# A hybrid attention and RWKV layer on one core: score pairs as 128-row matmuls with doubled keys, and a top-k search without 16-bit halves, three tiles of it counted on ScalarE

## The chip, the cores and the metric

The kernel runs on one core of one Trainium2 chip. A core has five engines with a queue each: TensorE (PE; PEld is its weight load), VectorE (DVE), ScalarE (ACT), GpSimd (POOL) and SyncE (SP), which issues most DMAs. The metric is device time in microseconds for one execution.

## The reference, cut to what matters

One layer over 1024 prompt frames and 32 sample frames, width 1024. Half of the heads do sparse attention, half RWKV-7; then an output projection and an MLP with 4096 hidden units. What the change touches is the sparse half: an indexer scores each query against the admissible keys, the best 256 keys are kept, and softmax attention runs over these.

```python
dots  = einsum('bthd,bsd->bths', qi, ki_all) * 64 ** -0.5        # 8 indexer heads, 64 wide
score = einsum('bths,bth->bts', relu(dots), wi)
score = where(admissible, score, -inf)                           # chunk-causal
_, idx = top_k(score, 256)
s = einsum('btkgd,btskd->btkgs', q, gathered_keys) * 64 ** -0.5  # 8 heads, 4 key heads
o = einsum('btkgs,btskd->btkgd', softmax(s), gathered_values)
```

## The kernel before

**Precision.** A float32 operand x is split into a high part `hi` (rounded to float32r, the matmul's input type) and a rest `lo = x - hi`; a product needs hi*hi + hi*lo + lo*hi. Head vectors are 64 long, so two of these fit on the 128 rows of the array.

**Tiles.** Tokens are in nine tiles: 0 to 7 are 128 prompt rows each, tile 8 is the 32 sample rows. Tile t has 128(t+1) keys, tile 8 has 544. Tiles 0 and 1 need no search, since all their keys are kept.

**Indexer** (`key_tile`, `key_T`, `cache_keys`, `idx_tile`). `key_T` transposes 64-wide keys and writes the high part to rows 0 to 63 and again to rows 64 to 127 of `kiA`/`ksA`, and the rest to the 64 rows of `kiB`/`ksB`. Queries `qs` hold the high part above the rest. For each of 8 heads and each 512 keys, L324 multiplies 128 rows (`qs` by `kiA`), L325 adds a 64-row matmul (high query by `kiB`); ScalarE applies relu (L326), VectorE weighs and sums over heads into `sc` (L330).

**Top-k search** (`topk`, `count`, `step`). The 256th largest score is found bit by bit: 31 steps, i = 30 to 0. A step counts for each tile how many scores lie below a candidate, then three small VectorE operations (L365, L366, L368) set or clear the bit. The tiles are in two sets, `SLS = ((2,3,4,5,8),(6,7))`, whose steps alternate. The first set is counted on VectorE (L341). The second is counted on VectorE in the 15 upper steps (i >= 16) and by Sign passes with a running sum on ScalarE (L363) in the 16 lower ones; it closes with one more count and two passes that settle the last unit. In the upper steps both sets read `S.upper`, bfloat16 copies of the scores' upper 16 bits (seven copies in `main2`, L519; their space lies in a pool that opens when the indexer's pools have closed).

**Projections beside the search.** `step(1)` advances both sets after each of 18 token tiles (`norm_tile`) and 14 channel blocks (`zs_block`). A channel block is 3 x 24 matmuls of 352 columns (L441) into two accumulators `acc`; ScalarE evacuates each twice (L450, L451); of the third one VectorE first takes two columns into `shl` (L446).

**Attention and RWKV** (`attn_all`, `rwkv_all`, generators that are advanced in turns). For each of 4 key heads and each tile: `prep` (when a new key set begins) transposes keys into `Ks`/`Kp` (high part above the rest), `query` makes `Q` (high part twice) and `Ql` (rest, 64 rows), `scores` does L1107 (128 rows) and L1108 (64 rows), mask and exponent, `turn` transposes the weights, `product` multiplies by values. RWKV's `lane_inverse` is a serial chain of small GpSimd operations (L837, L839).

**Order.** The program order is written by hand through these generators with priorities; a scheduler with a simulated timeline places the instructions in each engine's queue, and an engine takes its queue in order.

Of the kernel before, what the change touches and what calls it, by code (L numbers as in the profile page):

```python
# [74 lines left out]
def rows_of(t):  # L75
    return 128 if t < 8 else 32
# [21 lines left out]
def flat(a):  # L98
    return a.rearrange("p a b -> p (a b)")
# [51 lines left out]
def phase_a(S, pwx, pwy, pa, pi, px, xp, ps, late):  # L151
    nc, I, O = S.nc, S.I, S.O
# [83 lines left out]
    TK = []  # L236
    for SL in SLS:
# [5 lines left out]
        X.off = S.tk.tile([128, 2, len(SL)], F32, name="off" + str(len(SL)))  # L243
    S.upper = None
    ones = S.tk.tile([128, 1], F32, name="ones")
# [3 lines left out]
    kiA = pi.tile([128, 1024], F32R, name="kiA")  # L249
    kiB = pi.tile([64, 1024], F32R, name="kiB")  # L250
    ksA = pi.tile([128, 544], F32R, name="ksA")
    ksB = pi.tile([64, 544], F32R, name="ksB")

    KN = {}

    def key_T(A, B, col, src, r):
        pt = ps.tile([128, 512], F32, name="pt", bufs=2)
        nc.tensor.transpose(pt[:64, :r], src, S.ident[:r, :r])
        nc.scalar.copy(A[0:64, col:col + r], pt[:64, :r])
        nc.scalar.copy(A[64:128, col:col + r], pt[:64, :r])  # L260
        nc.vector.tensor_tensor(B[:, col:col + r], pt[:64, :r], A[0:64, col:col + r].bitcast(F32), op=ALU.subtract)

# [24 lines left out]
    def key_turn(t):  # L287
        r = rows_of(t)
        if t < 8:
            key_T(kiA, kiB, t * 128, KN.pop(t), r)  # L290
        else:
            key_T(ksA, ksB, 512, KN.pop(t), r)

    def cache_keys():
        for c in range(4):
            ck = pa.tile([128, 64], F32, name="ck", bufs=2)
            nc.sync.dma_start(ck, I["cache_kidx"][0, 0, c * 128:(c + 1) * 128])
            key_T(ksA, ksB, c * 128, ck, 128)

    def idx_tile(t, W):  # L300
# [16 lines left out]
        for h in range(8):  # L317
            w = iw[:r, t, h:h + 1]
            rl = late["pj"].tile([128, 1024], F32, name="rl", bufs=2)
            for c0 in range(0, n, 512):  # L320
                c1 = min(n, c0 + 512)
                pd = ps.tile([128, 512], F32, name="pd", bufs=6 - ACB)
                o = pd[:r, :c1 - c0]
                nc.tensor.matmul(o, qs[:, h // 2, h % 2, :r], A[:, c0:c1], start=True, stop=False)  # L324
                nc.tensor.matmul(o, qs[0:64, h // 2, h % 2, :r], B[:, c0:c1], start=False, stop=True)  # L325
                nc.scalar.activation(rl[:r, c0:c1], o, AF.Relu)  # L326
            if h == 0:
                nc.vector.tensor_scalar(sc[:r, :n], rl[:r, :n], w, None, op0=ALU.mult)
            else:
                nc.vector.scalar_tensor_tensor(sc[:r, :n], rl[:r, :n], w, sc[:r, :n], op0=ALU.mult, op1=ALU.add)  # L330
# [13 lines left out]
    def topk(X):  # L344
# [9 lines left out]
        for i in range(30, -1, -1):  # L354

            upper = i >= 16 and S.upper
            if X.exact or upper:
                count(X, ALU.is_lt, c_of, S.upper if upper else S.sc)
            else:
                for j, t in enumerate(X.SL):  # L360
                    r = rows_of(t)
                    n = S.sc[t].shape[1]
                    nc.scalar.activation(junk2[:r, :n], S.sc[t][:r, :n], AF.Sign, bias=c_of(j, r), scale=-1.0,  # L363
                                         accum_out=cnt[:r, j:j + 1])
            nc.vector.tensor_tensor(nac, cnt, X.off[:, 0] if X.exact or upper else X.off[:, 1], op=ALU.is_gt)  # L365
# [61 lines left out]
    def zs_block(i, W, o_, pool, mu1):  # L427
# [5 lines left out]
        for b, (o, n) in enumerate(TB):  # L433
# [10 lines left out]
            with S.tc.high_priority(EVP) if i in EVI else nullcontext():  # L444
                if b == 2:
                    nc.vector.tensor_copy(S.shl[:m, :, zc // 128 + (zc == 1600)], acc[:m, 319:352:32])  # L446
                if b in ZMD:
# [64 lines left out]
    def main2():  # L512
        S.upper, c = {}, 0
        for X in TK:
            for t in X.SL:
                n = S.sc[t].shape[1]
                S.upper[t] = junk2 if t == 7 else S.eqb[:, c:c + n]
                c += n * (t != 7)
                (nc.gpsimd.tensor_copy if t in UPP else nc.scalar.copy)(S.upper[t][:rows_of(t), :n], S.sc[t][:rows_of(t)].bitcast(BF16)[:, 1:2 * n:2])  # L519
        nc.gpsimd.memset(S.shl, 0.0)  # L520
# [531 lines left out]
def attn_all(S, ap, ps):  # L1052
# [6 lines left out]
    def prep(j, samp):  # L1059

        nt, n, sx = (5, 544, "s") if samp else (8, 1024, "p")

        kt, vt = S.kv.pop((j, samp), None) or attn_load(S, j, samp)
        A = ap.tile([128, n], F32R, name="K" + sx, bufs=1)
        for t0 in range(0, nt, 4):
            t1 = min(nt, t0 + 4)
            p = ps.tile([128, 512], F32, name="ptr", bufs=PTB)
            for t in range(t0, t1):
                r = 32 if t == 4 and samp else 128
                nc.tensor.transpose(p[0:64, (t - t0) * 128:(t - t0) * 128 + r], kt[:r, t], S.ident[:r, :r])  # L1070
            m = 32 if t1 == 5 else 512
            c = slice(t0 * 128, t0 * 128 + m)
            nc.scalar.copy(A[0:64, c], p[0:64, :m])
            nc.vector.tensor_tensor(A[64:128, c], p[0:64, :m], A[0:64, c].bitcast(F32), op=ALU.subtract)
        J[j, samp] = A, vt

    def query(k):
# [12 lines left out]
        w.Q = X = ap.tile([128, 2, 128], F32R, name="Q", bufs=2)  # L1090
        w.Ql = Y = ap.tile([64, 2, 128], F32R, name="Ql", bufs=2)
        src = p.rearrange("p (h q) -> p h q", h=2)[:, :, :r]
        nc.scalar.activation(X[0:64, :, :r], src, AF.Copy, scale=0.125)
        nc.scalar.activation(X[64:128, :, :r], src, AF.Copy, scale=0.125)
        nc.vector.scalar_tensor_tensor(Y[:, :, :r], src, 0.125, X[0:64, :, :r].bitcast(F32), op0=ALU.mult, op1=ALU.subtract)

    def scores(k, h):
        j, t = items[k]
        w = W[k]
        r, n, X = w.r, w.n, w.Q  # L1100
        A = J[j, t == 8][0]
        w.s[h] = s = ap.tile([128, 1024], F32, name="s", bufs=XPB)[:r, :n]
        m = w.m[:, h * 3:h * 3 + 2]
        for i, c0 in enumerate(range(0, n, 512)):
            c1 = min(n, c0 + 512)
            pd = ps.tile([128, 512], F32, name="pd", bufs=PDB)[:r, :c1 - c0]
            nc.tensor.matmul(pd, X[:, h, :r], A[:, c0:c1], start=True, stop=False)  # L1107
            nc.tensor.matmul(pd, w.Ql[:, h, :r], A[0:64, c0:c1], start=False, stop=True)  # L1108

# [310 lines left out]
def body(tc, I, O, dbg=None):  # L1420
# [4 lines left out]
    with pool(name="const") as cp, pool(name="dram", space=DRAM) as dp:  # L1425
# [18 lines left out]
        with pool(name="xnt") as xp, pool(name="psA", space=PSUM) as ps:  # L1444
# [103 lines left out]
```

## Time and profile before

| | |
|---|---|
| median of 3 runs | 1850.66 us (1846.62 to 1853.6) |
| profiled execution | 1847.36 us, span 1845.6 us |
| TensorE busy, share of the span | 1716.0 us, 93% |
| VectorE | 986.4 us, 53% |
| ScalarE | 674.8 us, 37% |
| GpSimd | 587.0 us, 32% |
| mean granted TensorE clock | 0.945 of full speed |

The span is from the first to the last instruction of the profiled execution. Busy shares are means over stages with different limits, so each stage is read by itself. "Idle before, releaser" in a group of instructions says what ended the waits of the engine just before them.

### The profile page before, as it was taken

How to read it: one execution, taken by the hardware profiler on the slowest of the kernel's cores; microseconds unless marked ns; L12 is line 12 of the kernel's file. 1: busy time of each engine (PE TensorE's matmuls, PEld its weight loads, DVE VectorE, ACT ScalarE, POOL GpSimd, SP SyncE). 2: the span in 40 equal slices, each digit the busy share in tenths (PEclk: the TensorE clock that was granted, in tenths of full speed). 3: DMA queues.
4: the chain of work that ended last, by engine and by line, in shares of the span. 5: the costliest groups of instructions: out<-in, count | busy, mean ns of one | idle time of the engine just before them, and what ended most of it. 6: DMA issues, size and time to landing. Idle time of an engine off the chain costs nothing.

```text
span 1845.6 us, 29489 instructions
## 1 busy us (share of the span) xinstructions
PE 1716.0 (93%) x11394; PEld 1489.6 (81%) x11394; DVE 986.4 (53%) x2127; ACT 674.8 (37%) x1469; POOL 587.0 (32%) x894
## 2 busy tenths in 40 slices
PE   7999978798669988999899999999999999999999
PEld 6666667797546666666657779999999999999998
DVE  6456599999988777686552543222222222222224
ACT  6455432367635453454641332121212121212120
POOL 7446463244345434055210113121212131313120
PEclk9999988899658897999989999999999999999999
DMA  7111011132311112041212532111111111111105
GB/s 215 47 35 33 33 58 57 54 109 60 89 38 19 27 38 53 14 115 47 60 46 85 155 108 80 40 52 41 52 40 52 41 52 40 52 41 52 41 17 165
DMA packets 180196, 113.08 MB, mean 61 GB/s; under 512 B 51392, under 2 KB 169240, under 8 KB 180056
## 3 DMA queue, kind: packets, MB, share of 16 engines
q1 hardware_dynamic: 171224, 106.87, 20.6%
q10 hardware_dynamic: 8832, 4.33, 0.8%
q8 instruction: 89, 1.46, 0.3%
q14 instruction: 51, 0.42, 0.1%
HBM read 86.16 MB, written 25.01 MB: 60 GB/s over the span
## 4 chain that ended last, share of the span: by engine, by line
PE 66%; DVE 17%; POOL 6%; issue 3%; DMA 3%; ACT 3%; SPq 1%; DVEq 0%; POOLq 0%; ACTq 0%
PE pd L1328 20%; PE pr L1348 10%; DVE AR L341 7%; PE acc L209 5%; PE pc L1348 5%; PE po L1348 5%; PE po L1146 3%; POOL Yl L839 2%; POOL tl L837 2%; PE pd L325 2%; PE pd L1264 2%; PE ptr L1131 2%; DVE L L832 2%; PE pd L1108 1%; PE pd L324 1%
## 5 line engine op out<-in xcount | busy, mean ns | idle before, releaser
L1328 PE MATMUL pd<-hh,w1h 128*128 128x352 f32 x768 | 248.1, 323 | 2.4 <-issue 1.6
L1328 PE MATMUL pd<-hh,w1l 128*128 128x352 f32 x768 | 247.7, 323 | 0.7 <-DVE w1l L1195 0.7
L1328 PE MATMUL pd<-hl,w1h 128*128 128x352 f32 x768 | 247.0, 322 | 0.0
L1334 DVE TENSOR_TENSOR h2l<-rl,h2h 128x352 fp32r<-128x352 f32 x96 | 56.9, 593 | 275.7 <-ACT h2h L1333 275.7
L1332 POOL TENSOR_TENSOR rl<-rl 128x352 f32<-128x352 f32 x96 | 85.2, 888 | 214.0 <-ACT rl L1331 214.0
L1194 ACT CAST w2h<-w2r 128x512 fp32r<-128x512 f32 x64 | 39.7, 621 | 293.6 <-PE po L1348 144.7
L1328 PEld LDWEIGHTS pd<-hh,w1h 128*128 128x128 f32 x768 | 144.3, 188 | 3.0 <-issue 1.9
L1328 PEld LDWEIGHTS pd<-hh,w1l 128*128 128x128 f32 x768 | 144.3, 188 | 0.9 <-DVE w1l L1195 0.9
L1328 PEld LDWEIGHTS pd<-hl,w1h 128*128 128x128 f32 x768 | 144.9, 189 | 0.0
L1195 POOL TENSOR_TENSOR w2l<-w2r,w2h 128x512 fp32r<-128x512 f32 x32 | 41.6, 1299 | 299.8 <-ACT w2h L1194 289.3
L1348 PE MATMUL pr<-h2h,w2l 128*128 128x352 f32 x384 | 124.5, 324 | 0.0
L1348 PE MATMUL pr<-h2h,w2h 128*128 128x352 f32 x384 | 124.4, 324 | 0.0
L1348 PE MATMUL pr<-h2l,w2h 128*128 128x352 f32 x384 | 124.3, 324 | 0.0
L1354 DVE TENSOR_TENSOR ya<-ya,pr 128x352 f32<-128x352 f32 x84 | 43.8, 521 | 100.6 <-PE pr L1348 100.6
L1331 ACT ACTIVATE rl<-pd 128x352 f32<-128x352 f32 x96 | 44.3, 463 | 141.4 <-PE pd L1328 136.1
L1146 PE MATMUL po<-ph,vp 128*64 128x256 f32 x288 | 85.1, 418 | 2.1 <-DVE t L1154 1.6
L1131 PE MATMUL ptr<-ident,s 128*128 128x128 f32 (+2 forms) x328 | 66.6, 308 | 19.0 <-ACT s L1113 17.3
L837 POOL TENSOR_TENSOR tl<-L,Yl 128x56 f32<-128x56 f32 (+22 forms) x155 | 64.4, 416 | 61.6 <-DVE L L832 50.6
L341 DVE TENSOR_SCALAR_CACHE_REDUCE AR<-KB,cnd 128x384 bf16<-128x384 bf16 (+2 forms) x90 | 78.9, 877 | 1.2
L441 PE MATMUL acc<-xh,whx 128*128 128x352 f32 (+2 forms) x168 | 58.4, 348 | 19.3 <-ACT tm L451 12.0
L1333 ACT CAST h2h<-rl 128x352 fp32r<-128x352 f32 x96 | 46.6, 485 | 75.3 <-POOL rl L1332 75.3
L1131 PEld LDWEIGHTS ptr<-ident,s 128*128 128x128 f32 (+2 forms) x328 | 40.5, 155 | 39.9 <-ACT s L1113 18.8
(458 smaller groups left out, 4677.8 us busy)
## 6 DMA issues: line engine op xcount, KB each, us to landing
w1r<-in_w_ff_dram SPq DMA_DIRECT2D x32, 512.0 KB, 4.2
w2r<-in_w_ff_dram SPq DMA_DIRECT2D x64, 256.0 KB, 2.9
zsd<-zm SPq DMA_DIRECT2D x12, 528.0 KB, 3.0
wraw<-in_w_in_dram SPq DMA_DIRECT2D x24, 256.0 KB, 2.7
wraw<-in_w_in_dram SPq DMA_DIRECT2D x40, 128.0 KB, 2.5
x<-in_x_prompt_dram SPq DMA_DIRECT2D x8, 512.0 KB, 5.3
hres<-hd ACTq DMA_DIRECT2D x16, 256.0 KB, 3.0
out_dram<-hres SPq DMA_DIRECT2D x16, 256.0 KB, 2.4
```

What stands on the lines that cost most here:

```text
L209: nc.tensor.matmul(acc[:r, :n], l, w[:, :n], start=(i == 0), stop=(i == 23))
L341: nc.vector.tensor_scalar(junk[:r, :n], sc[t][:r, :n], get(j, r), None, op0=op, op1=ALU.add, accum_out=X.cnt[:r, j:j + 1])
L441: nc.tensor.matmul(acc[:m, :n], l, x, start=(j == 0), stop=(j == 23))
L837: eng.tensor_tensor(t_, L[:, 0:j, j:j + 1].to_broadcast([128, j, w]), Y[:, j:j + 1, m:16].to_broadcast([128, j, w]), op=ALU.mult)
L1131: nc.tensor.transpose(p[:x, i, h, :r], w.s[h][:, c0 + i * 128:c0 + i * 128 + x], S.ident[:r, :r])
L1146: nc.tensor.matmul(po, V[:x, kt], hi[:x, i, :, :r], start=(kt == 0), stop=(kt == w.nk - 1))
L1328: nc.tensor.matmul(acc, a[:, k], m[:, k, o:o + n], start=(i == 0), stop=(i == 23))
L1331: nc.scalar.activation(rl, acc, AF.Relu)
L1332: nc.gpsimd.tensor_tensor(rl, rl, rl, op=ALU.mult)
L1333: nc.scalar.copy(h2h[:, o:o + n], rl)
L1334: nc.vector.tensor_tensor(h2l[:, o:o + n], rl, h2h[:, o:o + n].bitcast(F32), op=ALU.subtract)
L1348: nc.tensor.matmul(acc, a[:, k], m[:, o:o + n], start=(i == 0), stop=(i == 11))
```

## The change

It has five parts. (1) Keys are doubled along the row axis before the transpose (for a computed tile by a GpSimd copy `k2`, for cached indexer keys by a second DMA), so that `kiA`/`ksA` and `K` hold the high part in both halves and `kiB`/`ksB` and `Kl` hold the rest in both halves; the second matmul of a score pair then has 128 rows, with the same stationary operand as the first, and adds rest by rest too. (2) Attention's `Q` holds the high part above the rest, `Ql` and one ScalarE copy go; `K` and `Kl` are one buffer each for sample and prompt. (3) The search reads float32 scores in all steps; `S.upper` and its copies go. (4) Tile 5 moves to the second set, which is counted on ScalarE in all 31 steps. (5) The `shl` copy moves from VectorE to ScalarE.

```diff
     def key_T(A, B, col, src, r):
         pt = ps.tile([128, 512], F32, name="pt", bufs=2)
-        nc.tensor.transpose(pt[:64, :r], src, S.ident[:r, :r])
-        nc.scalar.copy(A[0:64, col:col + r], pt[:64, :r])
-        nc.scalar.copy(A[64:128, col:col + r], pt[:64, :r])
-        nc.vector.tensor_tensor(B[:, col:col + r], pt[:64, :r], A[0:64, col:col + r].bitcast(F32), op=ALU.subtract)
+        nc.tensor.transpose(pt[:, :r], flat(src), S.ident[:r, :r])
+        nc.scalar.copy(A[:, col:col + r], pt[:, :r])
+        nc.vector.tensor_tensor(B[:, col:col + r], pt[:, :r], A[:, col:col + r].bitcast(F32), op=ALU.subtract)
...
     def key_turn(t):
         r = rows_of(t)
+        k2 = pa.tile([128, 2, 64], F32, name="ck", bufs=2)[:r]
+        nc.gpsimd.tensor_copy(k2, KN.pop(t)[:, None, :].to_broadcast([r, 2, 64]))
...
-                nc.tensor.matmul(o, qs[0:64, h // 2, h % 2, :r], B[:, c0:c1], start=False, stop=True)
+                nc.tensor.matmul(o, qs[:, h // 2, h % 2, :r], B[:, c0:c1], start=False, stop=True)
...
         for i in range(30, -1, -1):
-
-            upper = i >= 16 and S.upper
-            if X.exact or upper:
-                count(X, ALU.is_lt, c_of, S.upper if upper else S.sc)
+            if X.exact:
+                count(X, ALU.is_lt, c_of, S.sc)
             else:
...
-                    nc.vector.tensor_copy(S.shl[:m, :, zc // 128 + (zc == 1600)], acc[:m, 319:352:32])
+                    nc.scalar.copy(S.shl[:m, :, zc // 128 + (zc == 1600)], acc[:m, 319:352:32])
...
     def main2():
-        S.upper, c = {}, 0
-        for X in TK:
-            for t in X.SL:
-                n = S.sc[t].shape[1]
-                S.upper[t] = junk2 if t == 7 else S.eqb[:, c:c + n]
-                c += n * (t != 7)
-                (nc.gpsimd.tensor_copy if t in UPP else nc.scalar.copy)(S.upper[t][:rows_of(t), :n], S.sc[t][:rows_of(t)].bitcast(BF16)[:, 1:2 * n:2])
...
-        A = ap.tile([128, n], F32R, name="K" + sx, bufs=1)
+        A, B = [ap.tile([128, 1024], F32R, name=x, bufs=1)[:, :n] for x in ("K", "Kl")]
         for t0 in range(0, nt, 4):
...
+            r = 32 if t0 == 4 and samp else 128
+            k2 = ap.tile([128, 4, 2, 64], F32, name="k2", bufs=1)
+            nc.gpsimd.tensor_copy(k2[:r, :t1 - t0], kt[:r, t0:t1, None, :].to_broadcast([r, t1 - t0, 2, 64]))
             for t in range(t0, t1):
-                r = 32 if t == 4 and samp else 128
-                nc.tensor.transpose(p[0:64, (t - t0) * 128:(t - t0) * 128 + r], kt[:r, t], S.ident[:r, :r])
+                nc.tensor.transpose(p[:, (t - t0) * 128:(t - t0) * 128 + r], flat(k2[:r, t - t0]), S.ident[:r, :r])
...
         nc.scalar.activation(X[0:64, :, :r], src, AF.Copy, scale=0.125)
-        nc.scalar.activation(X[64:128, :, :r], src, AF.Copy, scale=0.125)
-        nc.vector.scalar_tensor_tensor(Y[:, :, :r], src, 0.125, X[0:64, :, :r].bitcast(F32), op0=ALU.mult, op1=ALU.subtract)
+        nc.vector.scalar_tensor_tensor(X[64:128, :, :r], src, 0.125, X[0:64, :, :r].bitcast(F32), op0=ALU.mult, op1=ALU.subtract)
...
-            nc.tensor.matmul(pd, w.Ql[:, h, :r], A[0:64, c0:c1], start=False, stop=True)
+            nc.tensor.matmul(pd, X[:, h, :r], B[:, c0:c1], start=False, stop=True)
...
-SLS = ((2,3,4,5,8),(6,7))
+SLS = ((2,3,4,8),(5,6,7))
```

## Rows read from the trace of the kernel before

**Rows 1.** Six stretches: length, busy time (instructions) per engine, granted clock, DMA share, GB/s.

```profile
84.00:232.00 148.00, 148.00 (x645) 97.67 (x644) 84.29 (x136) 75.02 (x161) 72.49 (x116) 1.00 0.11 31
232.00:358.00 126.00, 98.67 (x494) 89.34 (x493) 124.36 (x324) 30.90 (x66) 55.33 (x68) 0.86 0.19 58
358.00:475.00 117.00, 102.31 (x620) 98.67 (x619) 112.01 (x310) 87.22 (x183) 45.74 (x57) 0.98 0.26 76
475.00:568.00 93.00, 62.69 (x296) 49.51 (x296) 80.83 (x164) 45.48 (x106) 46.72 (x77) 0.56 0.23 59
568.00:1000.00 432.00, 400.29 (x3879) 279.67 (x3879) 285.52 (x657) 206.44 (x502) 146.89 (x305) 0.91 0.19 47
1000.00:1846.00 846.00, 835.99 (x5093) 816.00 (x5091) 253.83 (x426) 184.50 (x337) 169.25 (x153) 1.00 0.22 64
```

Busy times stand in the order PE, PEld, DVE, ACT, POOL.

**Rows 2.** Groups by line and shape, 232 to 475 us: ScalarE's first evacuation.

```profile
L450 ACT ACTIVATE zm<-acc,mu 128x352 f32<-128x352 f32 x36 | 19.7, 548 | 56.5 <-DVE shl L446 35.8 <-PE acc L441 20.7
```

**Rows 3.** Timeline of TensorE's matmuls in the indexer: start, duration, form.

```profile
187.24 0.39 PE L209 MATMUL acc<-wly,xh 128*128 128x512 f32 x1
187.47 0.40 PE L324 MATMUL pd<-kiA,qs 128*128 128x512 f32 x1
187.80 0.49 PE L325 MATMUL pd<-kiB,qs 64*128 64x512 f32 x1
188.22 0.51 PE L209 MATMUL acc<-why,xl 128*128 128x512 f32 x1
188.56 0.40 PE L209 MATMUL acc<-why,xh 128*128 128x512 f32 x1
```

**Rows 4.** Line L325, prompt tiles: durations, first and last start, forms.

```profile
L325 PE MATMUL pd<-kiB,qs x80: 322/492/502, 84.2 to 227.0; 64*128 64x512 f32 x48, 64*128 64x384 f32 x16, 64*128 64x128 f32 x8, 64*128 64x256 f32 x8
```

**Rows 5.** Groups by line and shape, 84 to 232 us: VectorE's widest head sum.

```profile
L330 DVE SCALAR_TENSOR_TENSOR G<-rl,iw,G 128x1024 f32<-128x1024 f32 x7 | 9.9, 1419 | 10.1 <-ACT rl L326 10.1
```

**Rows 6.** VectorE's busy time in counts (L341), sum over 84 to 568 us.

```profile
sum 484.00, DVE 174.36; mean DVE 43.59
```

**Rows 7.** Groups by line and shape, 232 to 475 us: counts, Sign passes, small operations.

```profile
L341 DVE TENSOR_SCALAR_CACHE_REDUCE AR<-AR,cnd 128x1024 bf16<-128x1024 bf16 x15 | 19.1, 1273 | 0.0
L363 ACT ACTIVATE AR<-G,cnd 128x1024 bf16<-128x1024 f32 x16 | 18.4, 1150 | 0.3
L341 DVE TENSOR_SCALAR_CACHE_REDUCE AR<-KB,cnd 128x896 bf16<-128x896 bf16 x15 | 17.0, 1136 | 0.0
L363 ACT ACTIVATE AR<-G,cnd 128x896 bf16<-128x896 f32 x16 | 16.7, 1043 | 25.0 <-DVE cnd L368 17.8 <-DVE nac L365 4.8 <-DVE shl L446 1.1
L341 DVE TENSOR_SCALAR_CACHE_REDUCE AR<-G,cnd 128x768 bf16<-128x768 f32 x16 | 16.2, 1010 | 0.3
L341 DVE TENSOR_SCALAR_CACHE_REDUCE AR<-KB,cnd 128x768 bf16<-128x768 bf16 x15 | 15.2, 1011 | 0.6
...
L368 DVE TENSOR_SCALAR cnd<-cnd 128x2 int32<-128x2 int32 x30 | 12.4, 415 | 0.0
...
L366 DVE SCALAR_TENSOR_TENSOR cnd<-nac,cnd 128x2 int32<-128x2 int32 x31 | 8.5, 274 | 0.0
...
L365 DVE TENSOR_TENSOR nac<-cnt,off 128x2 int32<-128x2 f32 x31 | 6.9, 223 | 0.4 <-ACT AR L363 0.3
...
L363 ACT ACTIVATION_READ_ACCUMULATOR AR<-G,cnd 128x1 f32 x32 | 6.1, 190 | 0.0
```

**Rows 8.** Groups by line and shape, whole span: attention's score pair, 512 columns.

```profile
L1108 PE MATMUL pd<-Kp,Ql 64*128 64x512 f32 x48 | 24.6, 536 | 1.6 <-DVE Ql L1095 1.6
...
L1107 PE MATMUL pd<-Kp,Q 128*128 128x512 f32 x48 | 23.0, 503 | 5.0 <-DVE bst L800 3.5 <-DVE m L1110 1.0 <-ACT Q L1094 0.5
```

**Rows 9.** Groups by line, GpSimd, 475 to 1000 us.

```profile
L839 POOL TENSOR_TENSOR Yl<-Yl,tl 128x56 f32<-128x56 f32 (+22 forms) x155 | 65.7, 424 | 10.7
L837 POOL TENSOR_TENSOR tl<-L,Yl 128x56 f32<-128x56 f32 (+22 forms) x155 | 64.4, 416 | 61.6 <-DVE L L832 50.6
...
L1231 POOL TENSOR_TENSOR tha<-kk,KB 128x512 fp32r<-128x512 f32 x2 | 2.5, 1294 | 1.2 <-DVE w L1231 1.2
```

More of the change, by code (lines that the diff above doesn't have):

```diff
@@ L243, in phase_a @@
         X.off = S.tk.tile([128, 2, len(SL)], F32, name="off" + str(len(SL)))
-    S.upper = None
     ones = S.tk.tile([128, 1], F32, name="ones")
@@ L249, in phase_a @@
     kiA = pi.tile([128, 1024], F32R, name="kiA")
-    kiB = pi.tile([64, 1024], F32R, name="kiB")
+    kiB = pi.tile([128, 1024], F32R, name="kiB")
     ksA = pi.tile([128, 544], F32R, name="ksA")
-    ksB = pi.tile([64, 544], F32R, name="ksB")
+    ksB = pi.tile([128, 544], F32R, name="ksB")
     KN = {}
@@ L288, in key_turn @@
         r = rows_of(t)
+        k2 = pa.tile([128, 2, 64], F32, name="ck", bufs=2)[:r]
+        nc.gpsimd.tensor_copy(k2, KN.pop(t)[:, None, :].to_broadcast([r, 2, 64]))
         if t < 8:
-            key_T(kiA, kiB, t * 128, KN.pop(t), r)
+            key_T(kiA, kiB, t * 128, k2, r)
         else:
-            key_T(ksA, ksB, 512, KN.pop(t), r)
+            key_T(ksA, ksB, 512, k2, r)
     def cache_keys():
         for c in range(4):
-            ck = pa.tile([128, 64], F32, name="ck", bufs=2)
-            nc.sync.dma_start(ck, I["cache_kidx"][0, 0, c * 128:(c + 1) * 128])
+            ck = pa.tile([128, 2, 64], F32, name="ck", bufs=2)
+            for i in range(2):
+                nc.sync.dma_start(ck[:, i], I["cache_kidx"][0, 0, c * 128:(c + 1) * 128])
             key_T(ksA, ksB, c * 128, ck, 128)
@@ L364, in topk @@
                                          accum_out=cnt[:r, j:j + 1])
-            nc.vector.tensor_tensor(nac, cnt, X.off[:, 0] if X.exact or upper else X.off[:, 1], op=ALU.is_gt)
+            nc.vector.tensor_tensor(nac, cnt, X.off[:, 0] if X.exact else X.off[:, 1], op=ALU.is_gt)
             nc.vector.scalar_tensor_tensor(cnd, nac, i, cnd, op0=ALU.logical_shift_left, op1=ALU.bitwise_xor)
@@ L1067, in prep @@
             p = ps.tile([128, 512], F32, name="ptr", bufs=PTB)
+            r = 32 if t0 == 4 and samp else 128
+            k2 = ap.tile([128, 4, 2, 64], F32, name="k2", bufs=1)
+            nc.gpsimd.tensor_copy(k2[:r, :t1 - t0], kt[:r, t0:t1, None, :].to_broadcast([r, t1 - t0, 2, 64]))
             for t in range(t0, t1):
-                r = 32 if t == 4 and samp else 128
-                nc.tensor.transpose(p[0:64, (t - t0) * 128:(t - t0) * 128 + r], kt[:r, t], S.ident[:r, :r])
+                nc.tensor.transpose(p[:, (t - t0) * 128:(t - t0) * 128 + r], flat(k2[:r, t - t0]), S.ident[:r, :r])
             m = 32 if t1 == 5 else 512
             c = slice(t0 * 128, t0 * 128 + m)
-            nc.scalar.copy(A[0:64, c], p[0:64, :m])
-            nc.vector.tensor_tensor(A[64:128, c], p[0:64, :m], A[0:64, c].bitcast(F32), op=ALU.subtract)
-        J[j, samp] = A, vt
+            nc.scalar.copy(A[:, c], p[:, :m])
+            nc.vector.tensor_tensor(B[:, c], p[:, :m], A[:, c].bitcast(F32), op=ALU.subtract)
+        J[j, samp] = A, vt, B
     def query(k):
@@ L1090, in query @@
         w.Q = X = ap.tile([128, 2, 128], F32R, name="Q", bufs=2)
-        w.Ql = Y = ap.tile([64, 2, 128], F32R, name="Ql", bufs=2)
         src = p.rearrange("p (h q) -> p h q", h=2)[:, :, :r]
         nc.scalar.activation(X[0:64, :, :r], src, AF.Copy, scale=0.125)
-        nc.scalar.activation(X[64:128, :, :r], src, AF.Copy, scale=0.125)
-        nc.vector.scalar_tensor_tensor(Y[:, :, :r], src, 0.125, X[0:64, :, :r].bitcast(F32), op0=ALU.mult, op1=ALU.subtract)
+        nc.vector.scalar_tensor_tensor(X[64:128, :, :r], src, 0.125, X[0:64, :, :r].bitcast(F32), op0=ALU.mult, op1=ALU.subtract)
     def scores(k, h):
@@ L1100, in scores @@
         r, n, X = w.r, w.n, w.Q
-        A = J[j, t == 8][0]
+        A, _, B = J[j, t == 8]
         w.s[h] = s = ap.tile([128, 1024], F32, name="s", bufs=XPB)[:r, :n]
@@ L1389 @@
 FOFF = -100
-UPP = ()
 EARLY = 0
@@ L1460, in body @@
             S.eq = [eq[:, i] for i in range(2)]
-            S.eqb = eq.rearrange("p a b -> p (a b)").bitcast(BF16)
             with pool(name="pq", side="right") as pq:
```

## The prediction

> **What bounds the kernel now.** I read the stretches first [rows 1]; their borders are where one group of matmul lines ends and the next begins. From 1000 us on TensorE is busy 836 of 846 us at the full clock with the output projection and the MLP. The change does not touch that, so I leave it at its time. The rest splits in four.
>
> 84 to 232 us, indexer scores (with token projections between them): TensorE is never idle, 148.0 of 148 us, at the full clock; VectorE does 84.3 us, ScalarE 75.0. TensorE sets the pace.
>
> 232 to 475 us, channel projection (L441) beside the bit-by-bit threshold search: VectorE is busy 236.4 of 243 us, TensorE 201.0 with the granted clock at 0.86 in the first half, ScalarE 118.1, of which only 30.9 in the first half. VectorE sets the pace. How a VectorE-bound search holds up TensorE is in the row of L450: ScalarE's evacuation of a projection block sat 35.8 us behind VectorE's small shl copy (L446), which stands in VectorE's queue behind counts [rows 2].
>
> 475 to 568 us, masks, first RWKV fronts and first scores: VectorE 80.8 of 93 us, clock 0.56. 568 to 1000 us, attention beside RWKV: TensorE 400.3 of 432 us, VectorE 285.5.
>
> **What the change costs and saves, part by part.** The sum is made against the profiled execution, 1847.4 us (span 1845.6), which lies 3.3 us under the median of the three runs.
>
> *A. Indexer's second matmul from 64 to 128 rows.* In a run of 128-row matmuls of 512 columns one starts every 0.23 us (187.24 to 187.47). Around a 64-row one the three starts are 0.33, 0.42 and 0.34 us apart: 1.09 us where three of 0.23 would take 0.70 [rows 3]. So a change to 64 rows and back costs about 0.39 us. There are 80 such matmuls with 128 query rows [rows 4]: 31 us. The 16 of the sample tile have half short moves; at an estimated 0.3 us they add 5. Upper bound 36 us, since TensorE has no gap to hide it in. Lower bound 0: VectorE and ScalarE could take over. With the stage at 112 us they would be busy 84.3 and 75.0 of it, 75% and 67%. Closest is the widest tile: VectorE needs 8 x 1.42 = 11.4 us for its eight heads [rows 5], TensorE 32 x 0.23 + 24 x 0.23 = 12.9 us for scores and one projection. TensorE stays ahead, narrowly; I take 28 of the 36.
>
> *B. The search.* VectorE: the counts take 174.4 us in all [rows 6]. A count of 768 elements takes 1.010 us on float32 and 1.011 us on the 16-bit half [rows 7], so leaving out the halves costs VectorE nothing per count. Here a rule speaks against the change. The Trainium skill (VectorE: DVE Perf Modes, "The perf-mode tier table") gives a bf16 tensor_scalar twice the speed of a float32 one. By it the exact set's 15 upper steps would have been half as dear in 16 bits, and the change would give back some 23 us of VectorE time (half of 15 x 3.1 us); these counts, which also accumulate, don't show it, and the measurement decides.
>
> What leaves VectorE: 15 upper steps of tiles 6 and 7, 15 x (1.136 + 1.273) = 36.1 us, and tile 5's 31 steps, 31 x 1.010 = 31.3 us; together 67. The three small operations of each step stay. What comes to ScalarE: 15 x (1.043 + 1.150) for tiles 6 and 7; 31 passes over tile 5's 768 elements at an estimated 0.94 us (0.107 us per 128 elements less than the 896 row); and 15 x 2 + 31 = 61 accumulator reads of 0.19 us [rows 7]. That is 32.9 + 29.1 + 11.6 = 74 us. The seven copies into halves go (an estimated 6 us at the price per element of a Sign pass), and 14 tiny shl copies come (14 x 0.2 = 3 us): +71 net.
>
> So the 243 us stage has, after the change: VectorE 236.4 - 67 = 169 us; ScalarE 118.1 + 71 = 189; TensorE 1008 L441 matmuls (14 blocks x 3 x 24) of 352 columns, at 0.23 x 352/512 = 0.16 us 162 us, and by the rows' remainder some 23 us of tail projections and first front matmuls, 185 in all. No engine needs more than 189 us, so at most 54 us go. In the half in which ScalarE already carried Sign passes TensorE was busy 102.3 of 117 us, 87%. With both engines near their load I expect about 90%: 189/0.9 = 210 us, a saving of 33. The lower bound is below nothing (first rival).
>
> The moved shl copy takes away a wait of ScalarE on VectorE. What is behind it in ScalarE's queue is the evacuation, and behind that TensorE, which has two accumulators. What is late next is the Sign passes: three in a row are 3.7 us with their reads, close to the 3.9 us (24 x 0.16) that a projection block takes.
>
> *C. After the search* the three-tile set needs for tile 5 a closing count and two more passes over 768 elements, each taken at the count's 1.0 us: 3 us, in a stretch that VectorE fills. Lower bound 0. I take +3.
>
> *D. Attention's second score matmul, 112 of them.* Their two records are 503 and 536 ns [rows 8], where an undisturbed 512-column record is about 400 [rows 3]: (0.10 + 0.14) x 112 = 27 us at most. The neighbours here are often other shapes (transposes, 64-row RWKV products), so many changes stay, and VectorE and RWKV chains also hold this stretch. I take 9; lower bound 0. One ScalarE copy per query tile goes as well, hidden by an engine that is busy 206 of 432 us.
>
> *E. Preparation of keys, eight times.* A GpSimd copy now stands ahead of the transposes, 128 x 512 for each group of four tiles; the nearest row, an operation on 128 x 512, is 1.29 us [rows 9]. Sample and prompt keys share one buffer, but the scores that read the old keys are issued before the next preparation, so I cost that at nothing. TensorE has RWKV work meanwhile. 8 x 0.5 = +4 us; from 0 (all hidden) up to the price of the slower rival below. The same doubling for the indexer (nine small copies, four more 32 KB loads, one ScalarE copy less per tile) lies ahead of 84 us beside GpSimd and TensorE work of the projections: nothing, and at the price of a whole step (1.3 us x 9) 12 us if all of that were exposed.
>
> Sum: -28 - 33 + 3 - 9 + 4 = -63. 1847.4 - 63 = 1784; with the median slightly above the profiled run, 1785 us.
>
> **The rivals.**
>
> *The Sign chain binds.* A step of the three-tile set is serial: 1.043 + 1.150 + 0.94 + 3 x 0.19 = 3.7 us on ScalarE, then 0.22 + 0.27 + 0.42 = 0.9 us on VectorE [rows 7]. If the rest of ScalarE's work in the stage ((118.1 - 41 - 6)/31 = 2.3 us a step) never falls into the gap, and each answer waits on average 1 us behind a count of the other set, a step takes 7.9 us: 31 x 7.9 = 245 us, and with an estimated 10 us before the first step and after the last the stage is 12 us longer than now. B turns from -33 to +12: 1785 + 45 = 1830 us. For it: both engines take work in order. Against it: the two sets alternate, and the second half already runs Sign passes with only 25 us of ScalarE waiting in 16 steps. 12 in 100.
>
> *The indexer's gain goes to VectorE*, which is near TensorE in the widest tiles, and the search behind it starts no earlier: A is 0, 1813 us. 12 in 100.
>
> *TensorE packs to its floor.* The exact set's search no longer needs the halves, so it can begin while the last indexer tiles still run; A reaches 36, B 54, D 9: -36 - 54 + 3 - 9 + 0 = -96, 1751 us. 18 in 100.
>
> *Slower: keys wait behind the lane inverse.* Its five passes keep GpSimd (64.4 + 65.7)/5 = 26 us each [rows 9]. A key copy queued behind a pass stops scores, and what follows them, until it ends. It decides from 63/8 = 8 us a preparation; with four of the eight behind a whole pass it is 4 x 26 = 104 us, 1889 us. Against it: small copies of the softmax sums already slip in between the passes' operations. 4 in 100.
>
> *Nothing changes*, because the stage after waits for something that none of this moves: 1847 us, 2 in 100.
>
> **How the numbers follow.** The forecast has 52 in 100; its own range, with A 18 to 36, B 20 to 45 and D 0 to 15, is 1765 to 1805 us. The 8-in-10 range runs from just under the floor case to between the two mild rivals, 1748 to 1822. Changes under 0.5% (9 us) can't be told from none here. Forecast, floor and the first two rivals are all faster by more than that; after a little off for what I don't see, faster 0.92, same 0.04, slower 0.04.
>
> **What would show it.** Right: the indexer stretch 20 to 36 us shorter with all its score matmuls at 0.23 us starts; counts on VectorE near 107 us; Sign passes on ScalarE near 115 us; no wait of L450 on VectorE; the last L441 matmul 50 to 70 us earlier than 471; the MLP untouched. Wrong: TensorE waiting for ScalarE between projection blocks as long as it waited before; VectorE full again in the search; TensorE idle at the key transposes behind GpSimd.

## The result and the profile after

The change took 3.0% off: 1793.8 us (median of 4 runs, 1787.85 to 1796.1) against 1848.6 beside it, ratio 0.970 with a 95% interval of 0.966 to 0.974. The profiled execution is the shortest of the four, 1787.85 us, span 1786.1. Times of a kernel as a whole and what an edit "costs" are medians; all times inside a kernel are from its profiled execution. The forecast was 1785, but its terms came out otherwise than its sum.

Six stretches of the changed kernel, with the columns of [rows 1]; the borders lie where the same work ends.

```profile
84.00:204.00 120.00, 117.21 (x652) 98.58 (x651) 85.33 (x130) 68.21 (x156) 87.61 (x114) 1.00 0.13 36
205.00:320.00 115.00, 99.49 (x571) 92.26 (x570) 108.32 (x290) 81.82 (x171) 60.64 (x77) 0.96 0.24 71
320.00:418.00 98.00, 87.40 (x533) 84.74 (x532) 72.46 (x198) 84.82 (x190) 43.66 (x52) 0.98 0.28 83
418.00:510.00 92.00, 52.90 (x223) 39.93 (x223) 71.89 (x150) 47.17 (x101) 52.83 (x79) 0.51 0.24 54
510.00:930.00 420.00, 380.38 (x3905) 275.16 (x3906) 301.69 (x689) 205.40 (x492) 151.29 (x319) 0.92 0.22 52
930.00:1786.00 856.00, 847.23 (x5139) 824.89 (x5137) 251.85 (x426) 182.79 (x334) 169.73 (x153) 1.00 0.21 62
```

The indexer is 27 us shorter, the projections beside the search 30 us (243 to 213), the stretch of the masks keeps its length (93 to 92), attention beside RWKV loses 12. From 930 on 10 us are given back: the MLP itself is untouched (757.7 us before, 757.4 now), but its first matmul comes 100 us after the end of attention and RWKV, 86 before.

Timeline of TensorE in the indexer, after (L325 and L326 are the score pair now), against [rows 3]:

```profile
181.96 0.40 PE L209 MATMUL acc<-why,xh 128*128 128x512 f32 x1
182.19 0.40 PE L325 MATMUL pd<-kiA,qs 128*128 128x512 f32 x1
182.43 0.40 PE L326 MATMUL pd<-kiB,qs 128*128 128x512 f32 x1
182.66 0.40 PE L325 MATMUL pd<-kiA,qs 128*128 128x512 f32 x1
182.89 0.39 PE L326 MATMUL pd<-kiB,qs 128*128 128x512 f32 x1
183.13 0.39 PE L209 MATMUL acc<-wly,xh 128*128 128x512 f32 x1
```

All starts are 0.23 to 0.24 us apart; the 0.33, 0.42 and 0.34 around a 64-row matmul are gone. From 84 to 204 us TensorE is idle for 2.8 us, of which it waits 2.7 for ScalarE's relu (L327); it was never idle before.

Groups by line and shape, after: ScalarE from 205 to 418 us, then VectorE from 205 to 510 us.

```profile
L362 ACT ACTIVATE AR<-G,cnd 128x768 bf16<-128x768 f32 x27 | 25.3, 936 | 32.8 <-DVE cnd L367 26.1 <-DVE cnd L353 3.3 <-DVE nac L364 2.9
L449 ACT ACTIVATE zm<-acc,mu 128x352 f32<-128x352 f32 x36 | 19.6, 544 | 0.0
L362 ACT ACTIVATION_READ_ACCUMULATOR AR<-G,cnd 128x1 f32 x79 | 14.9, 189 | 0.0
...
L445 ACT COPY shl<-acc 128x2 f32<-128x2 f32 x12 | 1.7, 144 | 3.0 <-PE acc L440 3.0
```

```profile
L342 DVE TENSOR_SCALAR_CACHE_REDUCE AR<-G,cnd 128x640 bf16<-128x640 f32 x31 | 27.2, 876 | 0.7
...
L364 DVE TENSOR_TENSOR nac<-cnt,off 128x3 int32<-128x3 f32 x31 | 7.7, 248 | 16.6 <-ACT AR L362 16.6
```

The evacuation's wait for VectorE (35.8 us, [rows 2]) is gone. In its place ScalarE waits for VectorE's candidate (L367) and VectorE for ScalarE's pass (16.6 us): the round trip of a Sign step. Over the whole span the passes and reads keep ScalarE busy for 105.4 us (their records overlap and add up to 114.3; forecast 115) and the counts VectorE for 107.5 (forecast 107).

Groups by line over the whole span, after: attention's score pair and the key copy on GpSimd.

```profile
L1099 PE MATMUL pd<-K,Q 128*128 128x512 f32 (+4 forms) x112 | 46.5, 416 | 13.4 <-DVE Q L1087 9.7 <-DVE m L1102 3.7
...
L1100 PE MATMUL pd<-Kl,Q 128*128 128x512 f32 (+4 forms) x112 | 39.1, 365 | 0.0
```

```profile
L1062 POOL COPY k<-kp 128x512 f32<-128x512 f32 x8 | 4.9, 614 | 30.0 <-PE ptr L1064 30.0
...
L1062 POOL COPY k<-ks 128x512 f32<-128x512 f32 x4 | 2.5, 612 | 12.5 <-DMA ks<-in_cache_k_dram 8.5 <-issue 3.3 <-PE ptr L1064 0.7
```

A key copy takes 0.61 us, half of the 1.29 it was bounded by [rows 9].

This table follows the work by times that I read from the traces (us; the experiments are explained below). Steps are VectorE's L364, RWKV's first chunk is VectorE's first copy of a chunk's result (L882), and attention and RWKV end with VectorE's last product before the output (L1146, and the last line of `rwkv_norm`).

| | before | after | old search | shl on VectorE | short Sign chain | two tiles, early |
|---|---|---|---|---|---|---|
| last indexer matmul | 227.5 | 200.0 | 199.6 | 200.3 | 199.8 | 199.8 |
| last projection matmul | 471.3 | 415.6 | 437.4 | 423.2 | 408.6 | 412.8 |
| last step of the search | 466.4 | 459.5 | 436.9 | 461.5 | 369.4 | 469.1 |
| last mask written | 519.4 | 506.1 | 488.7 | 516.1 | 432.2 | 496.6 |
| first attention scores | 506.8 | 449.5 | 476.1 | 459.9 | 448.2 | 448.2 |
| RWKV's first chunk | 587 | 568 | 558 | 571 | 539 | 551 |
| attention ends | 1001.6 | 907.6 | 935.4 | 929.4 | 926.1 | 901.3 |
| RWKV ends | 967.9 | 928.6 | 935.5 | 939.1 | 910.6 | 902.1 |

In the column of the short Sign chain the last step is one of VectorE's set; the Sign set's last is at 325 there. From before to after, the last projection matmul comes 56 us earlier, the last mask only 13. From its first pass at 208.6 us to its last step at 459.4 the three-tile set takes 8.1 us a step; the set on VectorE is done at 373 us, and its masks (tiles 2, 3, 4 and 8) are complete at 406.

### The profile page after: what moved, and what is told of

Same layout as the page of the kernel before. It is cut to its first block, busy times and chain, and to the rows that moved or that the text cites. A ratio compares the mean times of both kernels' runs of the same rounds, so it can differ in the third digit from the quotient of the medians.

```text
span 1786.1 us, 29443 instructions
## 1 busy us (share of the span) xinstructions
PE 1653.3 (93%) x11394; PEld 1475.2 (83%) x11394; DVE 938.7 (53%) x1996; ACT 712.9 (40%) x1549; POOL 619.7 (35%) x919
## 4 chain that ended last, share of the span: by engine, by line
PE 62%; DVE 13%; ACT 5%; POOL 3%; issue 3%; DMA 3%; SPq 0%; DVEq 0%; ACTq 0%; POOLq 0%
PE pd L1320 20%; PE pr L1340 10%; PE pc L1340 5%; PE po L1340 5%; PE po L1138 3%; PE pd L1256 3%; DVE AR L342 2%; ACT AR L362 2%; PE pr L1256 2%; DVE L L824 2%; PE ptr L1123 2%; PE pr L712 1%; POOL Yl L831 1%; PE pd L1099 1%; DVE cnd L367 1%
## 5 line engine op out<-in xcount | busy, mean ns | idle before, releaser
L362 ACT ACTIVATE AR<-G,cnd 128x768 bf16<-128x768 f32 (+2 forms) x93 | 96.7, 1040 | 43.0 <-DVE cnd L367 35.5
L1105 ACT ACTIVATE s<-s,m 32x544 f32<-32x544 f32 (+8 forms) x72 | 55.4, 770 | 72.4 <-DVE m L1102 60.2
L1123 PE MATMUL ptr<-ident,s 128*128 128x128 f32 (+2 forms) x328 | 62.5, 294 | 11.7 <-ACT s L1105 7.5
L1340 PEld LDWEIGHTS pr<-h2l,w2h 128*128 128x128 f32 x384 | 72.3, 188 | 0.1
```

The costliest lines, as they stand in the source:

```text
L1105: nc.scalar.activation(s, s, AF.Exp, bias=m[:, i:i + 1], scale=-1.0, accum_out=w.m[:, 6 + h:7 + h])
L1123: nc.tensor.transpose(p[:x, i, h, :r], w.s[h][:, c0 + i * 128:c0 + i * 128 + x], S.ident[:r, :r])
L1340: nc.tensor.matmul(acc, a[:, k], m[:, o:o + n], start=(i == 0), stop=(i == 11))
```

## Experiments

Each kernel is the changed one with one edit, unless said otherwise. Ratios are to the kernel before, run beside it; "costs" are differences of medians to 1793.8. The runs of one kernel differ with the mean granted clock that they got: over 58 runs of 13 kernels 0.01 of the clock goes with 12 us, so a few us between two kernels say nothing. Where an estimate "at equal clock" is given, it is worked out with this slope from the mean clocks of the runs; whether an edit itself lowers the clock isn't told apart by it.

### Parts undone

**e1: the indexer's second matmul on 64 rows again (part A).**

```diff
-nc.tensor.matmul(o, qs[:, h // 2, h % 2, :r], B[:, c0:c1], start=False, stop=True)
+nc.tensor.matmul(o, qs[0:64, h // 2, h % 2, :r], B[0:64, c0:c1], start=False, stop=True)
```

> The changed kernel with the indexer's second matmul back on 64 rows (the high query by the rest of the keys; the keys stay doubled, rest by rest is left out as before the change). Theory: the change of row count is what the indexer stretch lost; it comes back at once, 96 visits at 0.3 to 0.39 us, so the last indexer matmul ends some 27 us later and the whole takes 1794 + 27 = 1821 us. Rival: the search behind it would have absorbed it (VectorE or ScalarE set the end of that stage), 1794 to 1800 us.

Measured: 1818.9 us, ratio 0.982 (0.977 to 0.987), 25 us more. The last indexer matmul is at 230.9 us, and everything behind it is shifted by 29 to 33 us (in the profiled executions, where the changed kernel's is its shortest). Part A is confirmed in place and size.

**e2: attention's second matmul on 64 rows (part D).**

```diff
-nc.tensor.matmul(pd, X[:, h, :r], B[:, c0:c1], start=False, stop=True)
+nc.tensor.matmul(pd, X[0:64, h, :r], B[0:64, c0:c1], start=False, stop=True)
```

> The changed kernel with attention's second score matmul back on 64 rows (high query by the rest of the keys). Theory: attention is shorter by it, but the RWKV chain now ends that stretch, so the whole moves little: 1794 to 1801 us. Rival, by the prediction's term D: TensorE's order sets the stretch and it costs 9 to 27 us, 1803 to 1821 us.

Measured: 1830.3 us (runs at 1818.5, 1818.9, 1841.7 and 1842.0), ratio 0.988 (0.980 to 0.996). My theory fell: the part is worth 25 us by the two shorter runs alone, some 18 at equal clock (0.942 in these two, 0.948 on the mean in the changed kernel). Groups by line, whole span, of this kernel:

```profile
L1100 PE MATMUL pd<-Kl,Q 64*128 64x512 f32 (+4 forms) x112 | 51.5, 459 | 0.0
L1099 PE MATMUL pd<-K,Q 128*128 128x512 f32 (+4 forms) x112 | 51.0, 455 | 10.4 <-DVE Q L1087 8.7 <-DVE m L1102 1.6
```

The pair's busy time is 102.5 us against 85.6, and the matmuls' row count changes 179 times more at scores (233 against 54, counted over TensorE's order of starts; 199 in the kernel before).

**f1: the kernel before with attention's doubling alone (parts D and E).** The diff of `prep`, `query` and `scores` of the change, nothing else.

> The kernel before with parts D and E of the change alone (attention's keys doubled, second score matmul on 128 rows; indexer, search and shl as before). Before is 1848 to 1851 us. Theory: in before's order attention ends the stretch behind the search (its last product at 1001.6 us, RWKV's at 967.9), so shorter score pairs show at the end; undoing this part in the changed kernel cost 25 to 36 us, here the gain is 15 to 30 us: 1820 to 1835 us. Rival (the prediction's own terms, D -9 and E +4): 1843 to 1847 us. Second rival: attention alone pays nothing without the shorter indexer and the shared end, within 4 us of before.

Measured: 1847.8 us (10 runs), ratio 0.999 (0.996 to 1.002): nothing, and my theory fell. Row changes at scores fall from 199 to 59 and no time comes of it. Windows of this kernel's profiled execution, to set beside [rows 1]:

```profile
475.00:568.00 93.00, 58.68 (x255) 48.46 (x256) 77.80 (x154) 40.09 (x88) 47.26 (x70) 0.52 0.23 58
568.00:1000.00 432.00, 389.06 (x3866) 280.89 (x3866) 285.41 (x666) 199.60 (x480) 157.00 (x329) 0.89 0.18 45
```

TensorE is busy 11 us less from 568 to 1000, and its granted clock is 0.89 where it was 0.91; RWKV's first chunk came at 614 us instead of 587. (This execution is 10 us above the median of the ten, so its end says little.) The same second matmul is worth nothing in one order and 18 to 25 us in the other.

**e3: the old search (halves, tile 5 on VectorE, shl on VectorE), doubling kept.**

```diff
-            if X.exact:
-                count(X, ALU.is_lt, c_of, S.sc)
+            upper = i >= 16 and S.upper
+            if X.exact or upper:
+                count(X, ALU.is_lt, c_of, S.upper if upper else S.sc)
...
-SLS = ((2,3,4,8),(5,6,7))
+SLS = ((2,3,4,5,8),(6,7))
```

Left out here: the copies into halves, their buffer and the `shl` line, which go back as well.

> The changed kernel with the whole search of before (16-bit halves, tile 5 in the exact set, shl on VectorE); doubled keys and 128-row matmuls stay. Theory: the two parts add; the search's part is the 28 us by which the projection stretch got shorter, so 1794 + 28 = 1822 us, and VectorE is full again from 205 us on. Rival: the saved indexer time alone lets the search begin earlier and the rest is slack, 1794 to 1805 us; other rival: the search's part is more than the projection stretch shows, 1835 us and more.

Measured: 1801.8 us, ratio 0.973 (0.968 to 0.977): the whole of part B is worth 8 us, not 28 (5 by the ratios, whose intervals overlap; no run of the one kernel lies among those of the other). In the table: the projections end 22 us later than with the new search, attention starts 27 us later and ends 28 later, but the masks are complete 17 us earlier and RWKV's first chunk comes 10 us earlier. RWKV, which ends last in the changed kernel, ends 7 us later here, and that is what the whole kernel feels.

**e4: shl back on VectorE, new search. e9: shl on ScalarE, old search (e3 with this one line left as the change has it).** The diff is e4's.

```diff
-nc.scalar.copy(S.shl[:m, :, zc // 128 + (zc == 1600)], acc[:m, 319:352:32])
+nc.vector.tensor_copy(S.shl[:m, :, zc // 128 + (zc == 1600)], acc[:m, 319:352:32])
```

> The changed kernel with only the shl copy back on VectorE. Theory: with counts taken off VectorE the 14 copies wait little, since its queue now holds three-us trains at most: 1794 to 1800 us. Rival: in-order waits behind counts are the main cause by which the search held up the projections, and they come back in good part: 1805 to 1820 us, with ScalarE's first evacuation waiting on VectorE for 20 us or more.

> Doubled keys and 128-row matmuls with the whole search of before, 16-bit halves included, and only the shl copy on ScalarE. Theory: the halves cost nothing by themselves, the shl copy is worth more with VectorE full than the 17 us it is worth in the new search: 1802 - 20 = 1782 us, about 12 us under the changed kernel, so of the change's search part only the shl copy pays. Rival: the projections are held up by VectorE in other ways too (norm tiles, evacuation behind it), 1797 to 1802 us.

Measured: e4 1810.5 us, ratio 0.980 (0.973 to 0.988), 17 us more; projections, masks and scores all come 8 to 10 us later. Two of its runs had clocks of 0.931 and 0.936; the two at 0.946 and 0.948 took 1803 us, 9 more than the change. The time is the rival's by the median, its sign isn't there: ScalarE's evacuations wait 7.1 us for VectorE, not 20. e9 1816.7 us, ratio 0.981 (0.978 to 0.985): 15 us more than e3, some 9 at equal clock (0.941 against 0.945), where I expected a gain. The copy pays on ScalarE only with the new search. Why it costs there with the old one is open; the projections end 6 us later and the lane inverse 24.

### What ends the search, and what the masks release

**f4: the 15 lower steps (i below 15) of the Sign set left out.** The thresholds of tiles 5, 6 and 7 stay coarse, and so do their masks.

```diff
         for i in range(30, -1, -1):
+            if not X.exact and i < 15:
+                yield
+                continue
```

> The changed kernel with the 15 lower steps (i below 15) of the second set, tiles 5, 6 and 7, left out: their thresholds stay coarse, so the output is not the reference's; everything after the search runs as before. Theory: the three-tile Sign chain, 8.0 us a step, sets the last mask (506 us), and the last mask sets RWKV's second unit, whose buffers it frees, and RWKV ends the stretch. Then the projection stretch gets no shorter below TensorE's own work, but the last mask comes 20 to 60 us earlier, RWKV's first chunk comes earlier by about as much up to 30 us, and the end is 15 to 35 us earlier: 1759 to 1779 us. Rival (the stretch is set by TensorE's work or by attention, not by the Sign chain): the end moves by less than 8 us, 1786 to 1800 us.

Measured: 1779.6 us, ratio 0.960 (0.956 to 0.964), 14 us less than the change (some 18 by the ratios), at the edge of the theory's range. The last mask comes 74 us earlier, but the projections only 7 and RWKV's first chunk 29. Before and after the edit, from the views by source line: the writes of the keys' buffer of RWKV's second unit in the changed kernel, 505 to 525 us,

```profile
L681 DVE TENSOR_TENSOR KB<-k,D x2: 1214/1218/1221, 515.4 to 517.7; 64x1024 f32<-64x1024 f32 x2
L681 DVE TENSOR_TENSOR KB<-tha,D x2: 1210/1214/1217, 516.5 to 518.9; 64x1024 f32<-64x1024 f32 x2
...
  POOL D L644: 11.7, 1
```

and the stretch of the masks in f4:

```profile
418.00:510.00 92.00, 65.63 (x308) 52.71 (x309) 68.83 (x141) 35.91 (x82) 46.79 (x81) 0.55 0.22 49
```

This buffer (`KB`) takes the place of the masks' work buffer `S.eq`, so it can't be written before the last mask is done with it. In e4, e5, e7, e10, f2 and f3 the writes start 0.1 to 0.7 us behind the end of the last mask, as here in e10 (the last two masks on ScalarE, then the writes):

```profile
L404 ACT ACTIVATE mb<-KB x2: 950/1004/1057, 491.0 to 495.5; 128x896 bf16<-128x896 f32 x1, 128x1024 bf16<-128x1024 f32 x1
L681 DVE TENSOR_TENSOR KB<-k,D x2: 1211/1268/1324, 496.7 to 499.2; 64x1024 f32<-64x1024 f32 x2
```

In the changed kernel they come 9 us behind it (506.1, 515.4), since VectorE, in the order of its queue, first waits for the lane inverse on GpSimd and takes its result; GpSimd in its turn waits 11.7 us for the writes. Timeline of VectorE at that place, the changed kernel, then f4:

```profile
508.25 4.55 DVE L835 STREAM_TRANSPOSE G<-Yl 32x512 f32<-32x512 f32 x4 [3.28 <-POOL Yl L831]
```

```profile
508.18 7.92 DVE L827 STREAM_TRANSPOSE L<-G 32x1024 f32<-32x1024 f32 x4
516.13 2.28 DVE L838 STREAM_TRANSPOSE G<-Yl 32x512 f32<-32x512 f32 x2
```

In f4 the writes come at 468 to 474 us and TensorE gets 13 us more work into the stretch. What is late next is VectorE: the first lane inverse is ready at 506 us, as before the edit (508), but VectorE turns to it at 516, behind 7.9 us of transposes for the next unit. In all 14 profiled executions RWKV's first chunk comes either 43 to 62 us behind the start of these writes or, where the lane inverse is taken late (before, e3, e9, f1, f4), 19 to 25 us behind that. So the Sign chain does hold RWKV back: its first chunk comes 29 us earlier for 74 us of the last mask, and RWKV ends 18 us earlier. Attention ends 18 us later than in the changed kernel (926 against 908) and is last now, which leaves some 14 at the end. That the buffer is the way by which the chain acts is read from these times; no run changes the buffer alone.

**e5: two tiles in the Sign set, no halves.** `SLS = ((2,3,4,5,8),(6,7))`.

> The changed kernel with tile 5 counted on VectorE again (sets 2,3,4,5,8 and 6,7), all steps on float32 scores. Theory: the second unit of RWKV reuses the buffers of the scores and waits for the last mask, and the last mask waits for ScalarE's serial chain, 8.0 us a step with three tiles (208 to 457 us). With two tiles a step loses 0.94 + 0.19 us and is about 6.8 us, 31 x 6.8 = 211 us, so the masks end some 30 us earlier than 506 us, and of that 10 to 25 us reach the end: 1769 to 1784 us. Rival: VectorE, with 31 us of counts more, is full again and holds up projections and masks: 1797 to 1810 us.

Measured: 1797.7 us, ratio 0.971 (0.968 to 0.974): no gain, against my theory; the time lies in the rival's range. The masks are complete at 497.0 us instead of 506.1 and RWKV's first chunk comes at 559, but VectorE's set now ends last (432 instead of 373), and attention, which begins with that set's tiles, has its first product scaled at 503 instead of 481 and ends at 954. Its first scores come at 458, but the mask that they need is complete at 466 only, and TensorE waits 8.0 us for VectorE at the second ones.

**e7: four steps of VectorE's set beside each of the last two indexer tiles.** `EARLY = 4`.

> The changed kernel with eight steps of the exact set's search placed beside the last two indexer tiles. Theory: the exact set is not the one that ends last; the ScalarE chain of the other set keeps its 8 us a step, masks end at 500 to 508 us as now: 1788 to 1798 us. Rival: both sets share VectorE's queue, so with the exact set ahead the ScalarE set's answers come at once, its step falls to 6.5 to 7 us and masks end 30 us earlier: 1765 to 1780 us.

Measured: 1793.4 us, ratio 0.969 (0.966 to 0.972): no change, as expected, but not by the way expected. The masks are not complete at 500 to 508 us but at 518: the Sign set starts behind the early steps, its first step ends at 238 instead of 212 us and its last at 477 instead of 459. Against that the projections end 7 us earlier, the first scores come 6 us earlier, and RWKV ends 3 us earlier. So a last mask 12 us later cost nothing on balance here.

**e10: both, two tiles and the early steps.**

> Tile 5 on VectorE again, all steps on float32, and eight steps of the exact set beside the last two indexer tiles. Theory: VectorE is the fuller engine now and about half idle in the indexer, so eight steps of 4.1 us moved there free up to 30 us of the stretch behind: 5 to 15 us under the same kernel without it, 1760 to 1775 us. Rival: the steps delay the indexer's own VectorE work and TensorE with it: no gain or a loss of up to 15 us.

Measured: 1771.5 us (1766.9 to 1773.8), ratio 0.957 (0.954 to 0.959). This beats both kernels, by 77 us and 22. The table shows both starts early at once: masks at 496.6, first scores at 448, RWKV's first chunk at 551 (attention's first product is scaled at 480). Attention and RWKV end together, at 901 and 902.

**f3: eight early steps instead of four. f2: e10 with two buffers for the doubled keys** (`k2`, `bufs=2`).

> The version with two tiles on ScalarE, with eight instead of four steps of the exact set beside each of the last two indexer tiles (four gave 1771.5 us, none 1797.7 us). Theory: VectorE still has room beside the indexer (85 us busy of 120), so the search ends another 5 to 15 us earlier, but with attention's first masks no longer the last thing, only part of it shows: 1758 to 1772 us. Rival: more counts in VectorE's queue hold up the indexer's head sums and with them TensorE: 1775 to 1795 us.

> The version with two tiles on ScalarE and four early steps (1771.5 us), with two buffers for the doubled keys k2 in place of one. In the changed kernel GpSimd's copy into k2 waits for the transposes of the last one and TensorE waited 34 us in 8 places at these transposes. Theory: TensorE has RWKV work queued in most of these places, so the second buffer gives 0 to 6 us: 1765 to 1772 us. Rival: the wait is exposed in full, 10 to 25 us: 1746 to 1761 us.

Measured: f3 1807.3 us, ratio 0.975 (0.972 to 0.979), 36 us more than e10, some 21 at equal clock (0.938 against 0.950). The steps (L364) from 240 to 300 us by source line, first e10, then f3 (128x5 is VectorE's set, 128x2 the Sign set):

```profile
L364 DVE TENSOR_TENSOR nac<-cnt,off x19: 144/166/761, 241.8 to 299.4; 128x5 int32<-128x5 f32 x10, 128x2 int32<-128x2 f32 x9
```

```profile
L364 DVE TENSOR_TENSOR nac<-cnt,off x11: 155/167/1355, 241.5 to 298.1; 128x5 int32<-128x5 f32 x10, 128x2 int32<-128x2 f32 x1
```

The indexer is no longer than in e10 (last matmul at 199.4), so the rival's place was wrong too. Sixteen early steps stand in VectorE's queue ahead of the Sign set's first; its steps begin at 297 instead of 252 us and end at 513 instead of 469, and the masks at 537. f2 1790.9 us (1781.2 to 1798.6), ratio 0.965 (0.959 to 0.971), 19 us more than e10, where I expected nothing or a gain. The expectation had read a wait the wrong way round: in the changed kernel it is GpSimd's copies that wait for TensorE's transposes (34.4 us in 8 places), and TensorE's matmuls wait 2.2 us for a copy, so there was little to give back. Its four runs had clocks of 0.933 to 0.949 against 0.949 to 0.953; its two runs at 0.945 and above are still 10 to 13 us slower. TensorE's order is another one from the first key sets on, and in the profiled execution attention ended 32 us later. Whether the order or the buffer did it stays open.

## Why the prediction came out

**A, right.** Forecast -28; the last indexer matmul moved by 27.4 us and undoing it costs 25. VectorE stayed behind TensorE (85.3 of 120 us): the rival that gives this gain to VectorE is out. Of the eight us taken off the bound of 36, TensorE's busy time between the first and the last indexer matmul accounts for four (143.3 us before, 111.7 now: 31.6, or 0.33 a visit), and its waits for ScalarE, not VectorE, for 2.7.

**B, mis-sized: -33 forecast, -8 measured (e3, which takes back C too).** The stretch it was reckoned on did shrink as forecast, by 30 us, and by the mechanism named: VectorE 181 of 213 us busy, ScalarE 167, no evacuation behind VectorE, TensorE's waits for ScalarE at the heads of the projection blocks 17 us instead of 28. The step that failed is the unspoken one behind "243 us stage": that all that follows, and with it the end, moves with the end of the projections. Attention does: in all 14 profiled executions its first scores come 34 to 40 us behind the last projection matmul, and of B's part (e3 against the change) it gets 27 us at its start and 28 at its end. RWKV has a second input, the last mask, by way of the buffer `KB`. The new search brings the masks later, not earlier: they come 13 us earlier than before, of which A alone brings 27 (e1 has the same search and ends its masks at 535 us, 16 later than before). So RWKV's first chunk comes 10 us later than with the old search; RWKV ends 7 us earlier all the same, and it is RWKV that ends last in the changed kernel, 21 us behind attention. Before, attention ended last, 34 us behind RWKV. I had also said that the last L441 would be 50 to 70 us earlier; 56 was right, and told of attention alone.

**From 1000 us on**, left at its time, the kernel took 10 us more. Where RWKV ends last (ten of the 14 profiled executions) the rest takes 857 to 863 us, where attention does (before, e5, f1, f4) 844 to 853. The sum had no term for the change of the chain that ends last.

**The Sign chain**, the first rival, gave 7.9 us a step; it is 8.1. Its arithmetic held, and so did the late end of the search (22 us later than before in e1, where the rival had 12); its conclusion did not: the chain ends 44 us after the projections and does not hold these back; it delays the masks. In this order 15 of its 31 steps are worth 14 to 18 us (f4).

**C** was too small to be seen apart: from the last step to the last mask it takes 47 us (53 before).

**D and E, -5 forecast.** Alone on the kernel before they are worth nothing (f1, between 7 us less and 3 more), as forecast; in the changed kernel undoing D alone costs 18 to 25 us (e2). With A and B at 33 us, the rest of the 55 us is 22, and it belongs to this stretch if the parts add; that they do is not shown (of B, `shl` alone costs 9 to 17 us undone, the whole 8). That the price is of this order and not of the matmul is shown; which wait makes the difference is not. E's copies were bounded at twice their time (0.61 us), and the slower rival, keys behind a lane inverse, did not come: the copies wait for TensorE's transposes (30.0 us in 8), and TensorE's matmuls at the transposes wait 2.2 us for a copy and, once, 4.8 us for GpSimd's chain.

**The sum** held by luck: if the parts add, B was 25 us too dear and D and E some 17 too cheap. By stretches the terms look better than they were (27 of 28 us in the indexer, 30 of 33 beside the search, in attention 12 where 5 were forecast, and 10 given back behind it, for which there was no term), since a stretch that shrinks need not pass its gain on. "TensorE packs to its floor" is out as a whole, though the one thing it named, a set that starts beside the last indexer tiles, is half of the version that won (e10).

On the rule weighed in B: the measurement after agrees with that before. A count of 640 elements takes 0.876 us on float32 here and took 0.875 on the 16-bit half (group by line and shape, before, 232 to 475 us):

```profile
L341 DVE TENSOR_SCALAR_CACHE_REDUCE AR<-KB,cnd 128x640 bf16<-128x640 bf16 x15 | 13.1, 875 | 0.1
```

So the halves bought nothing. The Trainium skill (VectorE: DVE Perf Modes, "The perf-mode tier table") gives a bf16 tensor_scalar twice the speed of a float32 one; that does not show in these accumulating counts.

On A, the Trainium skill (TensorEngine Tiling (Array Packing), "Key Properties") says that a change of the tiling mode drains TensorE; [rows 3] and the timeline after fit that, at 0.39 us for a visit to 64 rows and back in the rows shown.

## What to carry to other kernels

A stage's gain is what the chain that ends last gets of it. Before adding up stages, name for each later chain the instructions that release it, a reused buffer included, and say which chain ends last before and after; follow that one, not the engine that was busiest.

Two chains that start a stretch together (here VectorE's set for attention, the Sign set for RWKV) have to be shortened together: e5 and e7 alone gave nothing, both gave 22 us. And early work for one chain in a queue taken in order is a delay for the other one (f3).

An edit's price belongs to the order in which it was measured: the same matmul was worth nothing and 18 to 25 us.

## What was not expected of the hardware

- Runs of one kernel differ in time, and in granted clock with it, by more than many edits do: 0.01 of the mean clock goes with 12 us, and e2's runs range from 0.923 (1842 us) to 0.942 (1818.5).
- In f1's profiled execution 475 to 568 us ran at 0.52 instead of 0.56, and the 432 us behind it at 0.89 instead of 0.91, while TensorE was less busy. Whether the saved work or that execution brought the lower clock can't be told from it: the ten runs of f1 range from 0.932 to 0.947.
